# Partial sums of a five-tap convolution in a PSUM bank instead of SBUF

## The chip, the core and the metric

The kernel runs on one core of one Trainium2 chip. The metric is the device time of one execution in microseconds (us), and the median of three runs is compared. Four engines compute beside each other, each through its own queue in order: PE (matmuls, which write PSUM), DVE (element by element, reads and writes SBUF and PSUM), ACT (activations with a scale and a bias) and POOL (element by element, SBUF only). SP issues the DMAs. In the kernel's text they are `nc.tensor`, `V`, `A`, `P` and `nc.sync`.

## The reference

One layer of a hybrid block on x of 2048 x 1024 in float32. What the change touches is the centred depthwise convolution of the q, k and v columns:

```
mod = silu(c) @ ada_w + ada_b;  shift, scale, gate = split(mod)
h = rms_norm(x, norm_w) * (1 + scale) + shift
proj = h @ w_in                     # 1024 -> u 512, z_a 512, qkv 3 x 512, z_b 512, 16 gate columns
y_a = s5(u), gelu, GLU, * silu(z_a)           # diagonal state space, both directions
qkv = silu(conv(qkv, conv_w))       # 5 taps along the sequence, each channel by itself
q, k = l2_normalize(q) / sqrt(128), l2_normalize(k)
y_b = gated delta rule(q, k, v, g, beta), both directions, * silu(z_b)
out = rms_norm(x + gate * (concat(y_a, y_b) @ w_out), final_norm_w)
```

So for channel c and position t the convolution is the sum over j = 0..4 of conv_w[j, c] * raw[t + j - 2, c].

## The kernel before

The program has three stages. The first makes h, split into two float16 parts (`hhi`, `hlo`), and the four u column groups; the second, which is the one that matters here, makes the other columns of `proj` and the whole S5 scan beside them; the third runs the delta rule chunk by chunk with the GLU and the output projection beside it.

**The second stage.** `w_in` is taken in groups of 128 columns. A group is a *job* of four *iterations*, one per block of 512 positions. An iteration has one `gemm` on PE (24 matmuls of 128 x 512 into a bank with the tag `gm`) and one evacuation from that bank by ACT; then comes `tick()`, which emits what earlier iterations put off by `later(n, ...)`, and one step of the generator `side`, which is the S5 work. Nothing is reordered afterwards (`manual_schedule`): each engine's queue has the order in which the Python code emits. The jobs stand in the list `order` (line 182): z groups, the 16 gate columns, four k groups, four q groups, then v and z groups in turn.

**The convolution.** A k, q or v group goes through `conv_job`. With 512 positions of `raw` [128 channels x 2052 positions] written by ACT (L1017), these steps follow an iteration apart:

- `tap`: ACT writes a tile `cv` = conv_w[0] * raw (L1025);
- `conv`: DVE adds the taps 1 to 4 with four SCALAR_TENSOR_TENSOR (L1032), each `cv = raw[shifted] * conv_w[j] + cv`;
- `gated`: ACT applies silu in place (L1038) and squares (L1045);
- `total`, `taken`: PE sums the squares into a `pt` bank, DVE takes them (`kss` L1063 for k, `iq` L1059 for q);
- for k, after the fourth block, an inverse root of 13 small DVE operations (`rkt`, `rky`, `rk`), and then `turn` (PE transposes, L1075), `norm` (DVE, `kt`, L1085) and `back` (PE, L1092); for v only `turn`.

There are 12 such jobs, so 48 calls of `conv` and 192 SCALAR_TENSOR_TENSOR.

**The S5 work beside it.** At first it makes tables (`s5_tables`, eight times): POOL multiplies SBUF tiles (`bpw`, `cpw`, `tmp`; 12 operations of 128 x 512), PE transposes and multiplies into `sq` banks, ACT copies those out. Later come 16 batches of the scan, one step of `side` per iteration by turns: `s5_in` (PE into two `sq` banks, then four DVE products `w<-sq,rt`, then two POOL sums `w<-w,w`), and in the next iteration `s5_out` of the batch before (PE into two `sq` banks, `sq<-uT,tt` first, then ACT gelu) with `s5_scan` (four DVE scans `xs`, three DVE products, three POOL operations). POOL meanwhile makes `rt` tables for batches ahead.

**PSUM.** Eight banks: two with the tag `gm`, three `pt`, three `sq`. In this stage `sq` belongs to the S5 work alone. A tile is taken with `bank(tag)`, and whoever first writes it waits until the earlier user of that bank has been read to the end.

Of the kernel before, what the change touches and what calls it, by code (L numbers as in the profile page):

```python
# [31 lines left out]
def mm(nc, out, lhsT, rhs, start=True, stop=True):  # L32
    nc.tensor.matmul(out, lhsT, rhs, start=start, stop=stop)  # L33


def bc(ap, n):
    return ap.unsqueeze(2).to_broadcast([ap.shape[0], ap.shape[1], n])
# [3 lines left out]
def block(ctx, tc, x, c, ada_w, ada_b, norm_w, w_in, conv_w,  # L41
# [5 lines left out]
    V, A, P = nc.vector, nc.scalar, nc.gpsimd  # L47
# [39 lines left out]
    def bank(tag, shape=(128, 512)):  # L87
        return psum.tile(list(shape), F32, tag=tag, name=tag, bufs=PS_BUFS[tag])
# [19 lines left out]
    def rsqrt(pool, dst, src, tag):  # L108

        shp = list(src.shape)  # L110
        y = pool.tile(shp, F32, tag=tag + "y", name=tag + "y")
        t = pool.tile(shp, F32, tag=tag + "t", name=tag + "t")
        V.tensor_scalar(out=t.bitcast(I32), in0=src.bitcast(I32), scalar1=1, scalar2=None,
                        op0=ALU.arith_shift_right)
        V.tensor_scalar(out=y.bitcast(I32), in0=t.bitcast(I32), scalar1=-1.0,
                        scalar2=float(0x5F3759DF), op0=ALU.mult, op1=ALU.add)
        for it in range(3):
            V.tensor_tensor(out=t, in0=y, in1=y, op=ALU.mult)
            V.scalar_tensor_tensor(out=t, in0=t, scalar=-0.5, in1=src, op0=ALU.mult, op1=ALU.mult)
            V.scalar_tensor_tensor(out=(dst if it == 2 else y), in0=t, scalar=1.5, in1=y,  # L120
                                   op0=ALU.add, op1=ALU.mult)
# [52 lines left out]
    cw = s5t.tile([128, 12, 5], F32, name="cw")  # L174
# [798 lines left out]
    def later(n, fn, rank=0):  # L973
        late.append((clock[0] + n, fn, rank))
# [9 lines left out]
    def job(i, evac):  # L984
        w = w_done(i)
        for tb in range(NB):
            ps = gemm(w, tb)
            evac(tb, ps, w[2])
            if tb == 0:
                w_dma(i + 2)  # L990
                mx, cut = w_max(i + 1), w_cut(i + 1)
                next(mx, None)
            elif tb == 1:
                whole(mx)
            else:
                next(cut, None)
                next(cut, None)
            tick()
# [8 lines left out]
    def conv_job(i, kind, h):  # L1007
        i12 = kind * 4 + h
        raw = rp.tile([128, L + 4], F32, tag="big", name="raw")
        V.memset(raw[:, 0:2], 0.0)  # L1010
        V.memset(raw[:, L + 2:L + 4], 0.0)
        cvs = {}
        if kind == 1:
            ss, rk = [sp.tile([128, NCH], F32, tag=t, name=t, bufs=2) for t in ("kss", "rk")]

        def evac(tb, ps, iv):
            A.activation(out=raw[:, 2 + tb * 512:2 + (tb + 1) * 512], in_=ps, func=AF.Copy, scale=iv)  # L1017
            if tb:
                later(1, lambda: tap(tb - 1))
            if tb == NB - 1:  # L1020
                later(2, lambda: tap(tb))

        def tap(tb):
            cv = cvs[tb] = tp.tile([128, 512], F32, tag="cv", name="cv", bufs=9)
            A.activation(out=cv, in_=raw[:, tb * 512:tb * 512 + 512], func=AF.Copy, scale=cw[:, i12, 0:1])  # L1025
            later(1, lambda: conv(tb))

        def conv(tb):
            cv = cvs[tb]
            o = tb * 512  # L1030
            for j in range(1, 5):
                V.scalar_tensor_tensor(out=cv, in0=raw[:, o + j:o + j + 512], scalar=cw[:, i12, j:j + 1], in1=cv,  # L1032
                                       op0=ALU.mult, op1=ALU.add)
            later(1, lambda: gated(tb))

        def gated(tb):
            cv = cvs[tb]
            A.activation(out=cv, in_=cv, func=AF.Silu)  # L1038
            if kind == 0:
                nc.sync.dma_start(out=qT_d[:, tb * 4:tb * 4 + 4, h, :], in_=cv.rearrange("p (c t) -> p c t", t=128))  # L1040
            if kind == 2:
                later(1, lambda: turn(tb))
                return
            sq = tp.tile([128, 512], F32, tag="sq", name="sq")
            A.activation(out=sq, in_=cv, func=AF.Square)  # L1045
            later(1, lambda: total(tb, sq), 2)

        def total(tb, sq):

            ps = bank("pt")  # L1050
            for j in range(4):
                mm(nc, ps[:, j:j + 1], sq[:, j * 128:(j + 1) * 128], ones[:, 0:1])
            later(1, lambda: taken(tb, ps), 1)

        def taken(tb, ps):
            c4 = slice(tb * 4, tb * 4 + 4)
            if kind == 0:

                V.tensor_scalar(out=iq2[:, c4, h], in0=ps[:, 0:4], scalar1=EPS, scalar2=128.0 * EPS,  # L1059
                                op0=ALU.add, op1=ALU.mult)  # L1060
                cvs.pop(tb)
                return
            V.tensor_scalar(out=ss[:, c4], in0=ps[:, 0:4], scalar1=EPS, scalar2=None, op0=ALU.add)  # L1063
            if tb == NB - 1:

                rsqrt(sp, rk, ss, "rk")
                for n in range(NB):
                    later(1 + n, lambda n=n: turn(n), 2)

        def turn(tb):  # L1070
            c4 = slice(tb * 4, tb * 4 + 4)
            cv = cvs.pop(tb)
            ps = bank("pt")
            for j in range(4):
                nc.tensor.transpose(ps[:, j * 128:(j + 1) * 128], cv[:, j * 128:(j + 1) * 128], ident)  # L1075
            if kind == 2:
                vt = tp.tile([128, 4, 128], F32, tag="z", name="vt", bufs=3)
                A.activation(out=vt, in_=ps, func=AF.Copy)
                nc.sync.dma_start(out=vt_d[:, c4, h, :], in_=vt)
                return  # L1080
            later(1, lambda: norm(ps, c4), 1)

        def norm(ps, c4):
            kt = tp.tile([128, 4, 128], F32, tag="kt", name="kt", bufs=3)
            V.tensor_tensor(out=kt, in0=ps.rearrange("p (c d) -> p c d", d=128), in1=bc(rk[:, c4], 128), op=ALU.mult)  # L1085
            nc.sync.dma_start(out=kt_d[:, c4, h, :], in_=kt)
            later(2, lambda: back(kt, c4), 1.5)

        def back(kt, c4):
            ps = bank("pt")  # L1090
            for j in range(4):
                nc.tensor.transpose(ps[:, j * 128:(j + 1) * 128], kt[:, j, :], ident)  # L1092
            kk = tp.tile([128, 4, 128], F32, tag="z", name="kk", bufs=3)
            A.activation(out=kk, in_=ps, func=AF.Copy)
            nc.sync.dma_start(out=kT_d[:, c4, h, :], in_=kk)

        job(i, evac)
# [763 lines left out]
```

## Time and profile before

| | |
|---|---|
| median of 3 runs | 1428.95 us (1426.14 to 1430.29) |
| the profiled execution: time | 1428.77 us |
| its span, first to last instruction | 1427.1 us |
| its mean granted PE clock | 0.952 |
| busy in the span: PE, DVE, ACT, POOL | 1297.3, 1057.0, 672.9, 733.2 us |
| the taps (L1032), all 192 | 197.5 us of DVE, from 266.9 to 762 us |

The time lies 1.7 us over the span and 0.2 us under the median. The profile comes in views: the page (shares and the costliest groups of instructions), groups of instructions by line, one line's or tile's shortest, median and longest duration, the sum of each pair of "who waited for whom", stretches of the span with each engine's busy time, the instructions in order of time, and the chain of waits that ended last. A row of the page's groups reads: line, engine, operation, out<-in, shapes, count | busy us, mean ns | idle time just before them and what ended most of it. The granted PE clock is a share of full speed.

### The profile page before, as it was taken

The numbers are of one execution on the slowest core, as the hardware profiler recorded it, in microseconds if no ns is written. First come the engines' busy times: TensorE is split into PE (matmuls) and PEld (weight loads), VectorE is DVE, ScalarE is ACT, GpSimd is POOL, SyncE is SP. The second block draws the span as 40 slices with busy tenths as digits, with TensorE's granted clock in tenths as the row PEclk, the third lists the DMA queues.
The fourth block names the chain that finished last, engine by engine and source line by source line (L and its number), as shares of the span: only waits on it lengthen the run. The fifth ranks groups of instructions, "written<-read, shape, count | busy, mean of one in ns | idle before, by whom it ended". The sixth has DMA issues, their size and how long they took to land.

```text
span 1427.1 us, 26499 instructions
## 1 busy us (share of the span) xinstructions
PE 1297.3 (91%) x9936; PEld 907.2 (64%) x9936; DVE 1057.0 (74%) x2095; ACT 672.9 (47%) x1348; POOL 733.2 (51%) x680
## 2 busy tenths in 40 slices
PE   3879897797999998999999889999999988998997
PEld 2445343354565554555455578999999877886885
DVE  4645488988866799999984677887888665865664
ACT  4444321452455454353536666667667523433232
POOL 3223223685642367978761566655555125653543
PEclk9889998898999999999999899999999999999999
DMA  9455333122346623434324523543444489685533
GB/s 316 155 122 146 99 83 91 57 88 71 107 133 163 177 83 113 125 107 135 115 89 141 170 63 110 158 125 135 134 123 175 160 274 319 216 310 206 177 104 111
DMA packets 255280, 206.43 MB, mean 145 GB/s; under 512 B 88496, under 2 KB 206256, under 8 KB 255152
## 3 DMA queue, kind: packets, MB, share of 16 engines
q1 hardware_dynamic: 255152, 204.75, 46.4%
q8 instruction: 78, 1.28, 0.4%
q14 instruction: 50, 0.41, 0.1%
HBM read 133.38 MB, written 73.33 MB: 145 GB/s over the span
## 4 chain that ended last, share of the span: by engine, by line
PE 64%; DVE 21%; DMA 4%; issue 3%; ACT 3%; POOL 1%; SPq 1%; DVEq 0%; ACTq 0%; POOLq 0%
PE gm L33 36%; PE sq L33 15%; PE pt L33 12%; DVE cv L1032 6%; DVE w L510 2%; DMA y<-ya_d 1%; DVE xs L939 1%; DVE tm L510 1%; DVE wl L223 1%; PE pt L1075 1%; DVE t L510 1%; DMA kq<-qT_d 1%; DVE YT L1432 1%; DVE pb L1419 1%; PE sq L1748 1%
## 5 line engine op out<-in xcount | busy, mean ns | idle before, releaser
L33 PE MATMUL gm<-hhi,wh 128*128 128x512 f16 (+1 forms) x784 | 296.7, 394 | 13.0 <-ACT wh L221 6.9
L33 PE MATMUL gm<-hhi,wl 128*128 128x512 f16 (+1 forms) x784 | 294.9, 391 | 9.2 <-DVE wl L223 9.2
L33 PE MATMUL gm<-hlo,wh 128*128 128x512 f16 (+1 forms) x784 | 295.9, 393 | 0.0
L33 PEld LDWEIGHTS <-wh 128*128 128x128 f16 (+1 forms) x1664 | 154.4, 101 | 202.7 <-issue 30.9
L1032 DVE SCALAR_TENSOR_TENSOR cv<-raw,cw,cv 128x512 f32<-128x512 f32 x192 | 197.5, 1030 | 31.4 <-ACT cv L1025 26.3
L33 PEld LDWEIGHTS <-wl 128*128 128x128 f16 (+1 forms) x832 | 80.1, 100 | 109.2 <-DVE wl L223 12.6
L1017 ACT ACTIVATE raw<-gm,w 128x512 f32<-128x512 f32 x48 | 33.1, 689 | 180.9 <-PE gm L33 180.9
L510 POOL TENSOR_TENSOR w<-w,w 128x512 f32<-128x512 f32 x32 | 50.1, 1576 | 86.4 <-DVE w L510 86.4
L33 PE MATMUL gm<-yh,gwh 128*128 128x256 f32 x256 | 80.5, 315 | 6.7 <-ACT yh L778 5.4
L33 PE MATMUL gm<-yl,gwh 128*128 128x256 f32 x256 | 73.9, 289 | 0.7 <-POOL yl L779 0.7
L1770 POOL TENSOR_TENSOR r<-r,xt 128x512 f32<-128x512 f32 x32 | 41.5, 1297 | 62.2 <-DVE r L1769 29.1
L33 PE MATMUL gm<-yh,gwl 128*128 128x256 f32 x256 | 73.1, 285 | 0.0
L1440 ACT ACTIVATE Y<-pt 128x512 f16<-128x512 f32 x96 | 58.0, 604 | 24.5 <-PE pt L33 22.9
L939 DVE TENSOR_TENSOR_SCAN xs<-c,w 128x255 f32<-128x255 f32 x64 | 65.1, 1074 | 2.4 <-POOL w L510 2.4
L33 PE MATMUL sq<-S,kq 128*128 128x128 f32 x480 | 62.4, 282 | 0.0
L33 PEld LDWEIGHTS sq<-S,kq 128*128 128x128 f32 x480 | 60.0, 196 | 2.0
L1419 DVE CAST_PREDICATED pb<-msk,pt 128x512 f16<-128x512 int8 x80 | 57.0, 715 | 5.5 <-PE pt L33 4.4
L33 PE MATMUL pt<-Y,nh 128*128 128x64 f16 (+1 forms) x896 | 56.5, 198 | 4.6 <-DVE Y L1427 4.2
L320 POOL TENSOR_SCALAR hhi<-hf 128x512 f16<-128x512 f32 x32 | 30.1, 960 | 54.3 <-ACT hf L318 54.1
L1441 ACT ACTIVATE YT<-pt 128x512 f16<-128x512 f32 x96 | 57.3, 597 | 0.0
L33 PEld LDWEIGHTS <-nh 128*128 128x128 f16 x1024 | 48.2, 98 | 13.7 <-issue 6.6
L223 DVE SCALAR_TENSOR_TENSOR wl<-ws,w,wh 128x1024 f16<-128x1024 f32 (+1 forms) x25 | 36.2, 1448 | 27.6 <-ACT wh L221 27.6
(453 smaller groups left out, 3488.6 us busy)
## 6 DMA issues: line engine op xcount, KB each, us to landing
xt<-in_x_dram SPq DMA_DIRECT2D x25, 512.0 KB
ws<-in_w_in_dram SPq DMA_DIRECT2D x24, 512.0 KB
aw<-in_ada_w_dram SPq DMA_DIRECT2D x24, 512.0 KB
kq<-kT_d SPq DMA_DIRECT2D x32, 256.0 KB
kq<-qT_d SPq DMA_DIRECT2D x32, 256.0 KB
kt<-kt_d SPq DMA_DIRECT2D x32, 256.0 KB
vt<-vt_d SPq DMA_DIRECT2D x32, 256.0 KB
out_dram<-r SPq DMA_DIRECT2D x16, 512.0 KB
```

The source lines that it names most:

```text
L33: nc.tensor.matmul(out, lhsT, rhs, start=start, stop=stop)
L223: V.scalar_tensor_tensor(out=wl, in0=ws, scalar=s, in1=wh, op0=ALU.mult, op1=ALU.subtract)
L320: P.tensor_scalar(out=hhi[:, k, sl], in0=hf, scalar1=1.0, scalar2=1.0, op0=ALU.mult, op1=ALU.mult)
L510: (e or V).tensor_tensor(out=o, in0=a, in1=b, op=op)
L939: V.tensor_tensor_scan(out=o, data0=m1, data1=v, initial=0.0, op0=ALU.mult, op1=ALU.add)
L1017: A.activation(out=raw[:, 2 + tb * 512:2 + (tb + 1) * 512], in_=ps, func=AF.Copy, scale=iv)
L1032: V.scalar_tensor_tensor(out=cv, in0=raw[:, o + j:o + j + 512], scalar=cw[:, i12, j:j + 1], in1=cv, op0=ALU.mult, op1=ALU.add)
L1075: nc.tensor.transpose(ps[:, j * 128:(j + 1) * 128], cv[:, j * 128:(j + 1) * 128], ident)
L1419: V.copy_predicated(out=cols(PB[d][li], b, d), mask=mb, data=pp.rearrange("p t (n b) -> p t n b", b=b))
L1440: A.activation(out=cols(Y[d], b, d), in_=pa.rearrange("p t (n b) -> p t n b", b=b), func=AF.Copy)
L1441: A.activation(out=cols(YT[d], b, 1 - d), in_=pb.rearrange("p t (n b) -> p t n b", b=b), func=AF.Copy)
L1770: P.tensor_tensor(out=r[:, ns], in0=r[:, ns], in1=xt[:, ns], op=ALU.add)
```

## The change

`conv` takes a `sq` bank for each of its calls. Tap 1 reads `raw` and `cv` as before and writes the bank; taps 2 and 3 read `raw` and the bank and write the bank; tap 4 reads `raw` and the bank and writes `cv` in SBUF. Tap 0 by ACT (L1025) and everything behind `conv` stay.

```diff
         def conv(tb):
-            cv = cvs[tb]
+
+            cv, ps = cvs[tb], bank("sq")
             o = tb * 512
             for j in range(1, 5):
-                V.scalar_tensor_tensor(out=cv, in0=raw[:, o + j:o + j + 512], scalar=cw[:, i12, j:j + 1], in1=cv,
+                V.scalar_tensor_tensor(out=cv if j == 4 else ps, in0=raw[:, o + j:o + j + 512],
+                                       scalar=cw[:, i12, j:j + 1], in1=cv if j == 1 else ps,
                                        op0=ALU.mult, op1=ALU.add)
             later(1, lambda: gated(tb))
```

No instruction moves to another place or engine (behind the diff the line numbers are two higher). What changes is operands and waits. On DVE, at the second and third call of `conv` of the first k group (`kss` are the sums of squares, `w` a weight group's scale), before:

```order
L1010 MEMSET raw 128x2
L1011 MEMSET raw 128x2
L1032 SCALAR_TENSOR_TENSOR cv<-raw,cw,cv 128x512 [waits Activation_49]
L1032 SCALAR_TENSOR_TENSOR cv<-raw,cw,cv 128x512 [waits DVE_49] x3
L1063 TENSOR_SCALAR kss<-pt 128x4 [waits PE_49]
```

and with the change:

```order
L1010 MEMSET raw 128x2
L1011 MEMSET raw 128x2
L1033 SCALAR_TENSOR_TENSOR sq<-raw,cw,cv 128x512 [waits DVE_49,Activation_49]
L1033 SCALAR_TENSOR_TENSOR sq<-raw,cw,sq 128x512 [waits DVE_49] x2
L1033 SCALAR_TENSOR_TENSOR cv<-raw,cw,sq 128x512 [waits DVE_49]
L1065 TENSOR_SCALAR kss<-pt 128x4 [waits PE_49]
```

Each tap still waits for the one before it (DVE for itself); the first one now waits for the bank's earlier user too. On PE, at the start of `s5_out` of one batch (`uT`, `tt` and `cpt` are its inputs, `w` the scan's result), before:

```order
L33 MATMUL pt<-ones,sq 128x1 [waits DVE_49,Activation_49]
L33 MATMUL pt<-ones,sq 128x1 x3
L33 MATMUL sq<-uT,tt 128x256
L33 MATMUL sq<-uT,tt 128x256 [waits DVE_49,PE_49]
L33 MATMUL sq<-w_4813,cpt 128x256 [waits DMAHW4_49]
```

and with the change:

```order
L33 MATMUL pt<-ones,sq 128x1 [waits DVE_49,Activation_49]
L33 MATMUL pt<-ones,sq 128x1 x3
L33 MATMUL sq<-uT,tt 128x256 [waits DVE_49,PE_49]
L33 MATMUL sq<-uT,tt 128x256 [waits DVE_49]
L33 MATMUL sq<-w_4842,cpt 128x256 [waits DMAHW4_49]
```

With one of the three `sq` banks in the hands of `conv`, `s5_out` has to take both banks of the `s5_in` just before it, so its first matmul waits for DVE as well, where before only its second one did.

## The prediction

> **What bounds the kernel now.** The page gives the span and the group that the change touches, and the view by stretches says what its neighbourhood looks like. The columns of the latter: stretch, its length, busy time and count of PE, PE's weight loads, DVE, ACT and POOL, granted PE clock, share of the DMA engines, GB/s.
>
> ```profile
> span 1427.1 us, 26499 instructions
> L1032 DVE SCALAR_TENSOR_TENSOR cv<-raw,cw,cv 128x512 f32<-128x512 f32 x192 | 197.5, 1030 | 31.4 <-ACT cv L1025 26.3
> ...
> 480.00:570.00 90.00, 83.53 (x463) 46.80 (x462) 85.70 (x108) 41.85 (x69) 62.95 (x50) 0.94 0.33 99
> 570.00:710.00 140.00, 136.09 (x752) 71.65 (x752) 133.24 (x151) 62.72 (x101) 115.15 (x93) 0.98 0.39 117
> ```
>
> The taps lie between 266.9 and 762 us. There PE and DVE take turns as the bound: from 480 to 570 DVE is busy 85.7 of 90 us, from 570 to 710 PE is busy 136 of 140. A shorter DVE is therefore worth only what PE waits for it. The third view, PE's waits from 260 to 765 us (total us, times, longest):
>
> ```profile
> PE pt L1075 <- DVE kss L1063: 6.4, 2, 6.0
> PE gm L33 <- DVE wl L223: 6.1, 1, 6.1
> PE sq L33 <- DVE w L510: 5.2, 5, 3.1
> PE pt L33 <- DVE raw L1011: 3.0, 1, 3.0
> PE pt L1075 <- DVE iq L1059: 2.8, 1, 2.8
> PE pt L33 <- DVE iq L1059: 2.4, 1, 2.4
> PE pt L1075 <- DVE kt L1085: 1.9, 1, 1.9
> PE pt L1092 <- DVE kt L1085: 1.2, 1, 1.2
> ```
>
> All of them are for DVE, 29.0 us together. That is the frame: without its second-order effects the change cannot win more.
>
> **The change part by part.** *The four taps.* The fourth view, shortest/median/longest duration in ns by line, shows what a tap costs and why its mean of 1030 is so far over its median:
>
> ```profile
> L1032 DVE SCALAR_TENSOR_TENSOR cv<-raw,cw,cv x192: 740/752/1841, 266.9 to 761.2; 128x512 f32<-128x512 f32 x192
> L510 DVE TENSOR_TENSOR w<-sq,rt x64: 674/682/692, 483.2 to 742.8; 128x512 f32<-128x512 f32 x64
> L510 DVE TENSOR_TENSOR w<-xs,rt x32: 658/1040/1766, 494.4 to 751.6; 128x512 f32<-128x512 f32 x32
> L799 DVE SCALAR_TENSOR_TENSOR za<-gm,glub,za x32: 464/484/485, 810.4 to 1104.3; 128x256 f32<-128x256 f32 x32
> L1750 DVE SCALAR_TENSOR_TENSOR yb<-sq,dnw,zb x16: 739/744/752, 1200.5 to 1408.9; 128x512 f32<-128x512 f32 x16
> L510 POOL TENSOR_TENSOR bpw<-pwbr,bsi x7: 1054/1502/1506, 235.2 to 399.0; 128x512 f32<-128x512 f32 x7
> ```
>
> The same product in the same stage takes 674 to 692 ns in all 64 cases with one input in PSUM (`w<-sq,rt`), and 658 to 1766 with both inputs in SBUF (`w<-xs,rt`). POOL's operations, which read SBUF, stretch as well (1054 to 1506). So DVE and POOL get in each other's way where DVE reads two SBUF tiles, and not where one of them is in PSUM. Taps 2 to 4 change from the first kind to the second; tap 1 stays of the first. The chain of waits (start us, us) shows taps 2 to 4 of one call of `conv` in a collision, and from a later call one quiet tap:
>
> ```profile
> 313.98 1.65 DVE cv L1032
> ...
> 315.65 1.44 DVE cv L1032
> ...
> 317.11 1.43 DVE cv L1032
> ...
> 327.69 0.76 DVE cv L1032
> ```
>
> *What a tap will cost.* For reading PSUM the nearest row is `yb`: the same operation, size and kind of scalar, one input in PSUM, 744 against the tap's quiet 752; so nothing, or 8 ns less. No row shows a DVE write to PSUM, nor one that reads and writes the same bank. From below it is bounded by those 8 ns. From above I take once more all that an instruction costs beside its elements: 256 elements are 484 ns (`za`) and 512 are 744, so 260 per 256 elements, and 744 - 520 = 224 ns are fixed. I take nothing, because PSUM reading, the nearest row, costs nothing; both ends go into the range. A tap of the second kind is then 0.76 us with its gap, and a call like the one above saves 1.65 + 1.44 + 1.43 - 3 x 0.76 = 2.24 us.
>
> [...]
>
> *What the saving is worth, stall by stall.* Quiet calls save nothing. The calls behind PE's stalls, from the instructions in order of time:
>
> ```profile
> 266.88 5.34 DVE L1032 SCALAR_TENSOR_TENSOR cv<-raw,cw,cv 128x512 f32<-128x512 f32 x4
> 341.99 6.14 DVE L1032 SCALAR_TENSOR_TENSOR cv<-raw,cw,cv 128x512 f32<-128x512 f32 x4
> 377.45 6.14 DVE L1032 SCALAR_TENSOR_TENSOR cv<-raw,cw,cv 128x512 f32<-128x512 f32 x4
> 394.98 6.03 DVE L1032 SCALAR_TENSOR_TENSOR cv<-raw,cw,cv 128x512 f32<-128x512 f32 x4 [3.57 <-ACT cv L1025]
> ...
> 311.34 0.71 ACT L1025 ACTIVATE cv<-raw,cw 128x512 f32<-128x512 f32 x1
> ```
>
> - A, the 6.1 us for `wl` until 282.85: DVE works without a pause from the call at 266.88, which collides in taps 2 to 4: 2.2.
> - B, the 6.0 us for `kss` until 330.1: three colliding calls from 292 to 312 come before it, but PE waits for nothing there, and the fourth call cannot start before its tap 0 has left ACT at 311.34 + 0.71 = 312.05. So only the call of 312.49 counts, and the 0.4 by which it starts after 312.05: 2.6. Behind it come the 13 small operations of the inverse root.
> - C, 3.0 before 348.9 (call of 341.99): 2.2. D, 1.9 before 384.2 (call of 377.45): all 1.9. E, 1.2 before 401.7 (call of 394.98): all 1.2. What is late next in D and E is the evacuation of the `gemm` by ACT, which waits for PE itself.
> - F, 480 to 570, where DVE is the bound. Four calls recur (the row of 679 is for G, the last three are taps 2 to 4 of the call of 506.21):
>
> ```profile
> 485.85 4.52 DVE L1032 SCALAR_TENSOR_TENSOR cv<-raw,cw,cv 128x512 f32<-128x512 f32 x4
> 499.48 3.10 DVE L1032 SCALAR_TENSOR_TENSOR cv<-raw,cw,cv 128x512 f32<-128x512 f32 x4
> 506.21 4.94 DVE L1032 SCALAR_TENSOR_TENSOR cv<-raw,cw,cv 128x512 f32<-128x512 f32 x4
> ...
> 679.05 4.93 DVE L1032 SCALAR_TENSOR_TENSOR cv<-raw,cw,cv 128x512 f32<-128x512 f32 x4
> ...
> 508.00 1.00 DVE cv L1032
> 509.02 1.00 DVE cv L1032
> 510.05 1.10 DVE cv L1032
> ```
>
> The first saves 4.52 - 3.10 = 1.4 (its first tap is quiet), the second nothing, the third 1.00 + 1.00 + 1.10 - 3 x 0.76 = 0.8, the fourth collides in its first tap alone. Eight calls lie between 485 and 562: 2 x 2.2 = 4.4. PE's two waits for `iq`, 2.8 and 2.4, lie in this stretch and hold 5.2, so all of it counts.
>
> - G, the 3.1 for `w` until 697.5: one call like the third (4.93 us at 679) and one like the fourth: 0.8.
>
> The sum is 2.2 + 2.6 + 2.2 + 1.9 + 1.2 + 4.4 + 0.8 = 15.3 us, on 16 calls (one each in A, C, D, E, two in B, G, eight in F). The others, from 570 to 660 and from 710 on, lie beside PE at work; they save DVE time and no span. All taps together lie 197.5 - 192 x 0.752 = 53 us over their quiet time; three quarters of it, 40, are what DVE can save at most, so without PE's cover the others would be worth up to 25 us more.
>
> *The clock.* After a stall the `gemm` of 24 matmuls runs slower:
>
> ```profile
> 331.25 6.89 PE gm L33 x24
> ...
> 351.79 6.91 PE gm L33 x24
> ...
> 360.36 5.20 PE gm L33 x24
> ...
> 385.68 6.90 PE gm L33 x24
> ```
>
> The first, second and last stand behind B, C and D: 1.7 us each over the 5.20. C shrinks to 0.8 and D goes, B stays at 3.4. The two may be worth 3.4; I take 2.5.
>
> *The bank.* `conv` queues on DVE behind its tap 0 anyway; its bank was last used by itself, by DVE, or by S5 tiles that ACT read an iteration ago. So tap 1 does not wait. PE's first two matmuls of `s5_out`, 0.6 us, now stand behind the last of the four products of `s5_in` instead of before it:
>
> ```profile
> 523.85 0.68 PE L33 MATMUL sq<-uT,tt 128*128 128x256 f32 x2
> 524.75 0.67 PE L33 MATMUL sq<-uT,tt 128*128 128x256 f32 x2 [0.23 <-DVE w L510]
> ```
>
> That costs only where PE arrives before DVE is done, and where PE is the bound afterwards: at the ends of F and G and once near 630, 3 x 0.45 = 1.3. Behind these matmuls stand ACT's gelu and PE's next `gemm`; both are 0.45 later there, and nothing else waits for them.
>
> Together 15.3 + 2.5 - 1.3 = 16.5 us less than the profiled 1428.8: 1412.3. The median of the runs shown is 0.2 over it: 1412.5.
>
> **The rivals.** *The collisions move (1423).* POOL, no longer held up by taps, gets through its tables sooner and meets other DVE operations with two SBUF inputs: the scans, `w<-xs,rt`, the inverse root. For it: these stand right behind the taps in A, B and F. Against it: POOL also finishes sooner, so the total of shared time shrinks. If A, B and F give all back, 2.2 + 1.9 + 0.8 + 1.2 = 6.1 is left, less 1.3 for the bank and with 1 for the clock: 5.8, 1423.
>
> *A tap inside one bank is slow (slower, 1441).* If taps 2 and 3, which read and write one bank, take its elements twice (520 ns each) and a write costs the fixed 224 ns on three taps, a quiet call gets 1.7 us longer and a colliding one 0.5 shorter. Then A, C, D, E win 2.2; B loses 1.7 - 0.5 = 1.2; F loses 8 x 1.7 - 4.4 = 9.2; G loses 2 x 1.7 - 0.8 = 2.6; the bank 1.3: 12 us slower. It decides from 14 / 16 = 0.9 us per call. Against it: the `gemm` row above has PE add 24 times into one bank at 5.20 / 24 = 0.22 us per 512 columns, a reading and a writing each; DVE asks for less than half that pace.
>
> *More than the taps (1402).* POOL, less held up, leaves the neighbours alone: half of the 13.7 us of PE's waits that the sum leaves, 6.8, and all three slow `gemm`, 5.1: 15.3 + 6.8 + 5.1 = 27.2.
>
> *It does not do what it says (1430).* Taps 2 to 4 still read `raw` from SBUF and go on colliding: nothing but the bank's 1.3. The row `w<-sq,rt` speaks against it.
>
> **How the numbers follow.** The forecast (1405 to 1420) 0.60, collisions move 0.20, more 0.08, slow bank 0.07, no effect 0.05. The range reaches over the first and most of the second: 1404 to 1424; the upper bound of a PSUM write alone, 16 x 3 x 0.22 = 10.6, leads to 1423 and lies in it. A measurement here tells about 0.3%, 4.3 us, from no change, so faster is below 1424.7: 0.60 + 0.08 and 0.12 of the second case, 0.80. Same: 0.08 + 0.05 = 0.13. Slower: 0.07.
>
> **What would show it.** Taps 2 to 4 all near 750 ns with longest under 800, tap 1 still up to 1.8 us; DVE's tap time 40 us down at most, to 158, and rather less, since first taps collide oftener; POOL's longest `bpw` rows nearer to 1054. The stalls of C, D and E under 1 us and those of A and B at 3.9 and 3.4; 480 to 570 shorter by 4 to 5. PE's first `sq<-uT,tt` behind `w`. Wrong would be: taps 2 and 3 over 1 us without POOL at work, a wait of tap 1 for anything but ACT's tap 0, new waits of PE for taps, or stalls A to F as long as before with faster taps (then something else was the last to arrive).

## The result, and the profile after

The changed kernel takes 1407.01 us (median of 4 runs, 1399.43 to 1409.92) against 1427.55 (4 runs, 1423.39 to 1430.29) for the kernel before beside it: a ratio of 0.9852, 95% interval 0.9812 to 0.9892, or 15 to 27 us less. The prediction was 1412.5, with 1404 to 1424 as its range.

The profiled execution of the changed kernel is the fastest of its four, 1399.43 us. Where a size matters, the same kernel profiled once more is set beside it (called the repeat, 1408.24 us). First the taps, shortest/median/longest in ns, which answer to the row of L1032 before:

```profile
L1033 DVE SCALAR_TENSOR_TENSOR sq<-raw,cw,sq x96: 754/756/757, 268.5 to 730.2; 128x512 f32<-128x512 f32 x96
L1033 DVE SCALAR_TENSOR_TENSOR sq<-raw,cw,cv x48: 745/796/1844, 266.9 to 728.7; 128x512 f32<-128x512 f32 x48
L1033 DVE SCALAR_TENSOR_TENSOR cv<-raw,cw,sq x48: 747/748/749, 270.1 to 731.0; 128x512 f32<-128x512 f32 x48
```

Taps 2 and 3 (`sq<-raw,cw,sq`) and tap 4 (`cv<-raw,cw,sq`) have lost their spread altogether: the longest of 144 is 757 ns. Tap 1, which still reads two SBUF tiles, goes on colliding up to 1844. Next, PE's waits from 250 to 745 us (total us, times, longest):

```profile
PE gm L33 <- DVE wl L223: 6.0, 2, 5.1
PE pt L1077 <- DVE kss L1065: 3.9, 1, 3.9
PE sq L33 <- DVE cv L1033: 2.0, 2, 1.2
PE sq L33 <- DVE w L510: 1.9, 2, 1.2
PE pt L33 <- DVE raw L1011: 0.7, 1, 0.7
PE pt L1077 <- DVE iq L1061: 0.3, 1, 0.3
```

From 260 to 765 us, the stretch of the prediction's view, they are 13.9 us where there were 29.0 (0.9 of the first row lies ahead of it). Those of D and E (`kt`) are gone, those for `iq` in F nearly, C is at 0.7, G at most at 1.2; A and B are left at 5.1 and 3.9. The third row is new: PE waits for tap 4 to leave a bank. The `gemm` rows of the chain of waits that answer to those behind B, C and D (start us, us):

```profile
326.99 6.32 PE gm L33 x24
...
343.48 5.29 PE gm L33 x24
...
372.84 5.20 PE gm L33 x24
```

They were 6.89, 6.91 and 6.90. POOL's product `bpw<-pwbr,bsi`, which had a median of 1502, is quiet too:

```profile
L510 POOL TENSOR_TENSOR bpw<-pwbr,bsi x7: 1053/1055/1060, 234.6 to 384.1; 128x512 f32<-128x512 f32 x7
```

The quiet taps have not merely missed POOL's work. Before, 82 of the 192 taps took over 800 ns, all of them beside products of POOL (products of over 0.5 us, shared for over 0.2 us); of those not beside one, none took over 753. After, 67 of the 144 taps 2 to 4 still lie beside such products, and the longest of them took 757.

**Where the time went, by place.** The start of each iteration's `gemm` is a row of the trace; the difference of two such starts, before and after, says what the stretch between them won. From iteration 13 (250.43 us before) to iteration 80 (790.68), the second stage is 28.0 us shorter in the changed kernel and 25.2 in the repeat.

| place (iterations) | predicted | change | repeat |
|---|---|---|---|
| A, `wl` (13 to 18) | 2.2 | 0.85 | 0.6 |
| B, `kss` (18 to 23) | 2.6 | 2.1 | 2.5 |
| C (24 to 25) | 2.2 | 3.5 | 3.5 |
| a wait of 0.4 for `kss` (27 to 28) | 0 | 0.8 | 0.8 |
| D (28 to 29) | 1.9 | 2.1 | 2.1 |
| E (30 to 31) | 1.2 | 2.4 | 2.4 |
| F (44 to 51) | 4.4 | 6.7 | 4.1 |
| G (66 to 67) | 0.8 | 5.7 | 5.7 |
| slow `gemm` behind them | 2.5 | 5.4 | 4.5 |
| bank (55 to 56, 63 to 64) | -1.3 | -2.45 | -2.0 |
| a wait of 0.8 for `w` near 630 us (58 to 59) | 0 | 1.0 | 1.0 |
| sum | 16.5 | 28.0 | 25.2 |

The rest of the 29.3 between the two profiled executions, 1.3, lies ahead of iteration 13. The repeat is 20.5 us shorter in all: 25.2 in the stage, less 3.0 lost ahead of it and 1.6 behind iteration 80. The edit touches nothing there: these stretches differ by some us from one execution to the next. The kernel before was traced once, and some 2 us of the table are that execution's own, as the account of E in the section on why the prediction came out as it did shows.

### The profile page after: what moved, and what is told of

It is laid out like the page before. It is cut to its first block, busy times and chain, and to the rows that moved or that the text cites. A ratio compares the mean times of both kernels' runs of the same rounds, so it can differ in the third digit from the quotient of the medians.

```text
span 1397.7 us, 26524 instructions
## 1 busy us (share of the span) xinstructions
PE 1282.3 (92%) x9936; PEld 900.3 (64%) x9936; DVE 1017.6 (73%) x2095; ACT 672.5 (48%) x1348; POOL 708.1 (51%) x680
## 3 DMA queue, kind: packets, MB, share of 16 engines
q8 instruction: 78, 1.28, 0.4%
## 4 chain that ended last, share of the span: by engine, by line
PE 67%; DVE 16%; DMA 4%; issue 3%; POOL 3%; ACT 2%; SPq 1%; DVEq 0%; POOLq 0%; ACTq 0%
PE gm L33 37%; PE sq L33 15%; PE pt L33 12%; DVE sq L1033 2%; DVE w L510 2%; DVE tm L510 1%; DVE xs L939 1%; PE pt L1077 1%; POOL w L510 1%; DMA y<-ya_d 1%; DVE t L510 1%; PE sq L1750 1%; DMA xt<-in_x_dram 0%; DVE r L1782 0%; DVE cv L1033 0%
## 5 line engine op out<-in xcount | busy, mean ns | idle before, releaser
L1033 DVE SCALAR_TENSOR_TENSOR sq<-raw,cw,cv 128x512 f32<-128x512 f32 x48 | 55.2, 1151 | 29.6 <-ACT cv L1025 29.5
L1033 DVE SCALAR_TENSOR_TENSOR sq<-raw,cw,sq 128x512 f32<-128x512 f32 x96 | 72.6, 756 | 3.4
L939 DVE TENSOR_TENSOR_SCAN xs<-c,w 128x255 f32<-128x255 f32 x64 | 61.1, 1013 | 1.1 <-POOL w L510 1.1
L1003 ACT ACTIVATE z<-gm,w 128x512 f32<-128x512 f32 x32 | 22.0, 688 | 80.0 <-PE gm L33 48.0
```

Of the source, the lines that this page charges most:

```text
L939: V.tensor_tensor_scan(out=o, data0=m1, data1=v, initial=0.0, op0=ALU.mult, op1=ALU.add)
L1003: A.activation(out=z, in_=ps, func=AF.Silu, scale=iv)
L1033: V.scalar_tensor_tensor(out=cv if j == 4 else ps, in0=raw[:, o + j:o + j + 512], scalar=cw[:, i12, j:j + 1], in1=cv if j == 1 else ps, op ...
```

## The experiments

My theory: a tap is held up only while both it and an operation of POOL read SBUF with DVE reading two tiles there; taking one of DVE's inputs from PSUM ends that, and the price is what the bank costs. Rivals: it is the writing in place that matters, or any work of POOL; and for the path, that gains in one place are lost in another. All medians are beside runs of the kernel before on the same chip; "stage" is what the second stage won from iteration 13 to 80 in the profiled execution.

| form | median us | ratio, 95% interval | stage us |
|---|---|---|---|
| the change, repeated | 1405.0 | 0.9838, 0.9820 to 0.9855 | 25.2 |
| partial sums in a second SBUF tile | 1430.88 | 1.0025, 1.0012 to 1.0038 | 2.2 |
| taps in SBUF, bank taken anyway | 1432.69 | 1.0022, 1.0006 to 1.0038 | 0.0 |
| one immune tap | 1431.24 | 1.0028, 1.0015 to 1.0041 | 2.1 |
| one immune tap, bank kept | 1415.24 | 0.9900, 0.9872 to 0.9928 | 17.3 |
| POOL's table products as memsets | 1389.61 (one run) | | 35.2 |
| bank for k groups alone | 1414.86 | 0.9907, 0.9885 to 0.9929 | 16.8 |
| bank for q and v groups alone | 1420.63 | 0.9946, 0.9923 to 0.9969 | 14.0 |
| the change, bank kept | 1407.57 | 0.9846, 0.9821 to 0.9870 | 27.1 |
| tap 0 in the bank too | 1408.47 | 0.9849, 0.9827 to 0.9871 | 25.4 |
| tap 0 in the bank, k groups alone | 1401.98 | 0.9820, 0.9797 to 0.9843 | 31.6 |
| the same, bank kept for q and v | 1402.89 | 0.9814, 0.9789 to 0.9839 | 31.3 |

### The change, repeated

> The changed kernel once more, unaltered. It shows how far one execution's trace may be taken for all: the profiled one had 1399.4 us, its other runs 1406 to 1410. Expected: median 1403 to 1411, ratio to the kernel before 0.982 to 0.989. All 144 taps 2 to 4 at 747 to 757 ns again, whatever the total; a difference of the total then comes from stalls, not from taps. The rival, that the 1399 us were the rule and the others disturbed, expects a median under 1402.

The taps came out the same to the nanosecond (756, 748, first taps 1150 on average), the time 2 us lower. PE's waits for `wl` were 7.3 instead of 6.0 and those for `cv` 1.5 instead of 2.0, so an execution's own variation is about 1 us for a stall (in F, which holds several, 2.6).

### Is it the bank, or that the sum is not written in place?

```diff
-            cv, ps = cvs[tb], bank("sq")
+            cv, ps = cvs[tb], tp.tile([128, 512], F32, tag="pp", name="pp", bufs=1)
```

(and eight `cv` tiles instead of nine, to make room).

> The partial sums go to a tile of their own, but in SBUF (one buffer; the ring of cv has 8 in place of 9 to make room). Theory: a tap is held up because it reads two SBUF tiles while POOL reads SBUF, so a tile apart changes nothing: mean tap about 1030 ns, taps up to 1.6 us in positions 2 to 4, time within 0.3% of the kernel before (1423 to 1432 us). Rival: what cost was the sum in place (one tile read and written by one instruction); then the taps are near 750 ns and the time near 1407.

The groups of the taps, where `pp` is the second SBUF tile:

```profile
L1033 DVE SCALAR_TENSOR_TENSOR pp<-raw,cw,pp x96: 750/752/1652, 270.4 to 758.9; 128x512 f32<-128x512 f32 x96
...
L1033 DVE SCALAR_TENSOR_TENSOR cv<-raw,cw,pp x48: 750/752/1630, 273.5 to 759.7; 128x512 f32<-128x512 f32 x48
```

Taps 2 to 4 still collide, and tap 1 (between the two rows) with them; nothing is won. It is where the second input lies, not what is overwritten.

### What the bank alone costs

The four taps as before, all in SBUF, and two one-element writes of DVE into the bank, one ahead of the taps and one behind them:

```diff
+            V.tensor_scalar(out=ps[:, 0:1], in0=cw[:, i12, 0:1], scalar1=1.0, scalar2=None, op0=ALU.mult)
             for j in range(1, 5):
-                V.scalar_tensor_tensor(out=cv if j == 4 else ps, in0=raw[:, o + j:o + j + 512],
-                                       scalar=cw[:, i12, j:j + 1], in1=cv if j == 1 else ps,
+                V.scalar_tensor_tensor(out=cv, in0=raw[:, o + j:o + j + 512], scalar=cw[:, i12, j:j + 1], in1=cv,
                                        op0=ALU.mult, op1=ALU.add)
+            V.tensor_scalar(out=ps[:, 1:2], in0=cw[:, i12, 0:1], scalar1=1.0, scalar2=None, op0=ALU.mult)
```

> The taps stay in SBUF as before; conv takes an sq bank all the same, writes one element of it ahead of tap 1 and one behind tap 4 (two extra DVE operations of about 0.1 us per call). It measures the bank's loss from the rotation alone. Theory (the prediction's term): 1.3 us for PE's matmuls that stand behind conv's or s5_in's bank, and the 16 calls on the path bring 16 x 0.2 = 3 us with the extra operations: 1428 to 1434 us. Rival (the loss of a bank costs more than stated, and the gain of the taps is larger than the net result): 1436 us or more.

The interval of 0.06 to 0.38% over the kernel before is 1 to 5 us, the two small operations included (the one behind the taps took 147 to 155 ns). PE's waits show for what:

```profile
PE sq L33 <- DVE sq L1036: 6.0, 3, 3.6
```

So the bank's price is PE waiting for the end of a convolution that DVE has not reached. With colliding taps DVE is later, and the price higher, than in the change (2.0). The stage's 0.0 hides this: 2.3 us are lost at iteration 55, 4.2 at 63 and 1.3 at 64, and 5.7 are won at G, where the wait for `w` is gone because PE arrives later and not because DVE is faster. That a wait has gone is therefore no proof of faster taps; for G the form below that keeps one bank decides, which has no wait for a bank and wins the same 5.7.

### Does one immune tap do a third of it?

Tap 1 writes the bank, tap 2 reads it, taps 3 and 4 stay in SBUF; the bank is taken a call at a time, as in the change:

```diff
-                V.scalar_tensor_tensor(out=cv if j == 4 else ps, in0=raw[:, o + j:o + j + 512],
-                                       scalar=cw[:, i12, j:j + 1], in1=cv if j == 1 else ps,
+                V.scalar_tensor_tensor(out=ps if j == 1 else cv, in0=raw[:, o + j:o + j + 512],
+                                       scalar=cw[:, i12, j:j + 1], in1=ps if j == 2 else cv,
```

> Tap 1 writes the bank, tap 2 reads it and writes cv, taps 3 and 4 stay in SBUF. Theory: only a tap with an input in PSUM is immune, so tap 2 is at 745 to 760 ns in all 48 calls, taps 3 and 4 still collide (up to 1.6 us), mean over all four near 950. Since 2 of the 3 collisions stay, a third to a half of the gain: 1415 to 1422 us. Rival (the gain comes from the sum leaving SBUF as such, writes included): taps 3 and 4 get quiet too and the time is near 1407.

This missed. Tap 2 was immune (746 to 749 ns), taps 3 and 4 collided (mean 899), and by iteration 45 the kernel had won 9 us; at iteration 66 it was 3 behind. PE's waits say why, and one of them in PE's and DVE's rows:

```profile
PE sq L33 <- DVE cv L1033: 17.3, 6, 6.0
```

```profile
511.96 1.98 PE L33 MATMUL sq<-uT,bpt 128*64 128x256 f32 x8 [5.96 <-DVE cv L1033]
```

```profile
501.89 3.63 DVE L939 TENSOR_TENSOR_SCAN xs<-c,w 128x255 f32<-128x255 f32 x4
...
509.39 1.74 DVE L1033 SCALAR_TENSOR_TENSOR sq<-raw,cw,cv 128x512 f32<-128x512 f32 x1
511.16 0.75 DVE L1033 SCALAR_TENSOR_TENSOR cv<-raw,cw,sq 128x512 f32<-128x512 f32 x1
```

PE's second `s5_in` tile has the bank that this convolution uses, and starts when tap 2 has read it, at 511.91. DVE came to that convolution only after 7.6 us of scan and products. The bank that a tile gets is settled when the program is built, by the order in which the banks come free in its text. The order in the v groups (the numbers are banks, c marks a call of `conv`, the others are S5's tiles):

```
the change:       5c 4 5 3c 5 4 3c 5 4 3c 4 5 3 4 5 4 3
one immune tap:   5c 5 3 4c 3 5 4c 4 3 5c 3 4 5 3 4 3 5
```

With the bank free two taps earlier, the next S5 tile is given the very bank of the convolution before it (`5c 5`), in place of one that was free long since (`5c 4`).

The test of that reading keeps one bank for all 48 calls, so that none of S5's tiles ever gets it:

```diff
+    mine = []
...
+            if not mine:
+                mine.append(bank("sq"))
+            ps = mine[0]
```

> The form with one immune tap (tap 1 writes the bank, tap 2 reads it, taps 3 and 4 stay in SBUF), which had come out at 1431 with PE waiting 17.3 us for cv before its next tile in an sq bank; here the bank is taken once and kept for all 48 calls, so S5 never gets a bank that a tap still has to read. Theory (the 17.3 us came from which tile gets the early freed bank, not from the taps): those waits are gone, taps 3 and 4 collide as they did (mean about 900), and the 8 us that were won by iteration 45 stay: 1416 to 1422. Rival (one tap in the bank is worth nothing on the path, whichever bank): 1427 to 1432.

No wait of PE for `cv` is left, taps 3 and 4 collide as before (mean 901), and 1415.24 comes out, 0.8 under the theory's range. So one immune tap of three is worth 15 us, two thirds of the change, and all of it had been lost to who gets which bank.

### Is it POOL's reading?

The kernel before, with all taps in SBUF; in the S5 tables each of POOL's products is a memset of the same tile. The products of those tables are left out.

```diff
             for i in range(2):
+                if e is P:
+                    for u in (o[i], t, o[i]):
+                        P.memset(u, 0.01)
+                    continue
                 TT(o[i], a[0], b[i], ALU.mult, e)
```

> The form before (all taps in SBUF), with one thing changed: in the S5 table stage each of POOL's products of two 128x512 SBUF tiles is replaced by a memset of the same output tile, so POOL writes the same tiles at the same places and reads none. It leaves the products of the S5 tables out of the computation. Theory (a tap is held up where both it and POOL's operation READ two SBUF tiles): the 76 taps between 262 and 425 us, mean 1109 ns before, come down to about 755 (up to 800, for the few other POOL operations that stay), and the k part gets 13 to 17 us shorter, about 1411 to 1416 in all. Rival (any POOL work or POOL writing of SBUF stretches DVE): taps that lie beside a memset stay over 900 ns. Since a memset may be much shorter than a product (1.05 to 1.5 us), only taps beside a memset decide between the two, the total does not.

The taps from 255 to 425 us (98 of them; shortest/median/longest), and one call of four, whose first three taps have POOL's memsets of 0.52 us beside them, until 257.39:

```profile
L1036 DVE SCALAR_TENSOR_TENSOR cv<-raw,cw,cv x98: 743/752/1097, 255.2 to 424.4; 128x512 f32<-128x512 f32 x98
```

```profile
255.23 3.11 DVE L1036 SCALAR_TENSOR_TENSOR cv<-raw,cw,cv 128x512 f32<-128x512 f32 x4 [0.61 <-ACT cv L1029]
```

Of the 98 taps, 36 overlap a memset by more than 0.2 us, and the longest of these took 754 ns. Four are over 760, 991 to 1097 ns, and all four lie beside the products of 128x256 that POOL still had to do:

```profile
395.73 4.27 DVE L1036 SCALAR_TENSOR_TENSOR cv<-raw,cw,cv 128x512 f32<-128x512 f32 x4 [1.42 <-ACT cv L1029]
```

```profile
395.64 0.61 POOL L510 TENSOR_TENSOR qh<-rtA,rtB 128x256 f32<-128x256 f32 x1
...
398.38 1.07 POOL L510 TENSOR_TENSOR qh<-rtA,rtB 128x256 f32<-128x256 f32 x1
```

POOL's product is stretched as well: the first `qh`, which had begun before the taps, took 0.61 us, the second 1.07. So POOL's writing harms no tap (754 ns at most beside memsets); its products, which read SBUF as well, do (991 to 1097 ns beside those of 128x256), though not in every case: 17 more taps lie beside POOL's products of 128x16 (`l`, `lks`) and took at most 752 ns. There POOL alone paid, up to 0.71 us for a product that takes 0.22 elsewhere.

The total missed: 1389.6 against 1411 to 1416. The stage won 35 us, and the small DVE operations, which collide as well, have a part in it. Two of the inverse root's (it has eleven in the trace, not 13), before, and the first of them here (ns):

```profile
L118 DVE TENSOR_TENSOR rkt<-rky x12: 174/176/1128, 320.8 to 426.0; 128x16 f32<-128x16 f32 x12
...
L115 DVE TENSOR_SCALAR rky<-rkt x4: 175/577/979, 319.7 to 424.5; 128x16 int32<-128x16 int32 x4
```

```profile
L118 DVE TENSOR_TENSOR rkt<-rky x12: 174/175/176, 297.2 to 385.6; 128x16 f32<-128x16 f32 x12
```

An operation of 16 elements a row takes up to 950 ns longer beside POOL's products. The four long ones of `rkt` began 0.1 to 0.2 us behind the start of a product and ended 0.02 to 0.03 us behind its end, so they waited it out. `rky<-rkt` reads one SBUF tile and collides too, up to 979 ns before and 175 here: two SBUF inputs are what makes a tap collide, but not the only thing that makes a DVE operation collide. I had counted only taps. POOL's work is shorter as well (0.52 us for a memset where its products took 1.05 to 1.5), and what that alone is worth was not shown, so this run's total is no measure of the collisions alone.

### The k groups, and the q and v groups

```diff
-            cv, ps = cvs[tb], bank("sq")
+            cv, ps = cvs[tb], bank("sq") if kind == 1 else None
```

with `kind != 1` for the second form; without a bank the taps go as before.

> The bank for the partial sums in the four k groups alone (16 of 48 calls); q and v groups as before. Theory (each of the stalls A to E shrinks by what its own calls save, and the S5 stretch behind takes the lead over unchanged): 12 to 15 us of the gain are there by 410 us, the stretch from 480 on is as before, total 1412 to 1416. Rival (a lead won early is taken back in the stretch where DVE is the bound, as it was with one tap in the bank): 12 us at 410 us, but DVE waits longer there for nothing it can do, PE waits for it from 480 to 570, and the total is 1420 to 1427.

> The reverse: the bank in the q and v groups (32 calls), the k groups as before. Theory (stalls add up independently): nothing up to 400 us, then 4 to 7 us from 480 to 570 (F) and 5 to 6 us at the w products before 697 (G), less about 1 us for the bank: 8 to 11 us, total 1416 to 1419; together with the k groups' result the sum of the two gains is within 3 us of the whole change's 22. Rival (the gains depend on each other): the two sums differ from 22 by more than 5 us.

The two gains are 13.0 and 7.2 us by the medians, 20.2 together, against 22.1 for the change repeated; by the profiled stages 16.8 and 14.0, against 25.2 to 28.0. The profiled execution of the second form is at that form's median, 1420.63, so its smaller gain in the whole lies outside the stage (3.0 lost ahead of it and 2.9 behind). Its 1420.63 is 1.6 over the theory's range; the sum of the two gains is within the 3 us that the theory allowed, and by the stages 2.8 to 5.6 more than the change's. Some 2 of that is what the traced execution of the kernel before lost by itself (see E below), which counts in both. The waits of PE in the two forms stand each where its own groups are:

```profile
PE sq L33 <- DVE w L510: 4.7, 3, 3.1
...
PE pt L1077 <- DVE iq L1061: 2.8, 1, 2.8
```

```profile
PE gm L33 <- DVE wl L223: 7.0, 2, 6.1
PE pt L1077 <- DVE w L143: 6.0, 1, 6.0
```

With the bank for k alone, waits of F and G are those of the kernel before to the tenth (2.8 for `iq`, 3.1 for `w`), and the lead of 15.2 us that it has won by iteration 33 is 15.4 at iteration 51: a lead won early is not taken back. With the bank for q and v alone, A and B stand as before (6.1, and 6.0 in B's place).

### The bank kept, and tap 0 in the bank

*The change, bank kept for all 48 calls* (the same three lines as above).

> The change with one difference: one sq bank is taken at the first call of conv and kept for all 48, so S5 has the other two to itself, and no PE work ever waits for a tap; only DVE touches that bank, in its own order. Theory (what the shared bank costs is PE's waits for the last tap, 1.5 to 2.0 us, and about 1 us of them reaches the end): PE's waits for cv on sq banks are gone, taps as before (754 to 757, 748), PE waits a little longer for ACT or w with two banks, as it does now; 1402 to 1406. Rival (S5 needs the third bank: its pairs of PE tiles wait for the readers of the last pair): new waits of PE's sq tiles for DVE's w products or ACT's gelu over 5 us, 1409 to 1415.

PE's waits for `cv` are gone, and no wait for `w` or ACT grew (`w` 2.6 as in the repeat). The time, 1407.57, is 1.6 over the theory's range and not told from the change's: in the medians, the bank's price is too little to see. In the traces it can be read off. The repeat and this form agree in every iteration of the stage to 0.02 us but for 55 and 63, where the repeat is 0.99 longer each: 2.0 us, the difference between 25.2 and 27.1.

*Tap 0 in the bank too*, so that no DVE tap reads two SBUF tiles:

```diff
-            A.activation(out=cv, in_=raw[:, tb * 512:tb * 512 + 512], func=AF.Copy, scale=cw[:, i12, 0:1])
+            pss[tb] = bank("sq")
+            A.activation(out=pss[tb], in_=raw[:, tb * 512:tb * 512 + 512], func=AF.Copy, scale=cw[:, i12, 0:1])
```

> The change with ACT's tap 0 in the bank as well, so that all four DVE taps have one input in PSUM. Theory by the collisions alone: tap 1 falls from a mean of 1150 to about 756, 19 us less DVE time than in the change, the k part gains 2 to 4 us more; 1399 to 1403. Rival (bank release): each bank is now held from tap 0 to tap 4, an iteration longer, and where DVE is the bound (480 to 570 us before) PE's S5 tiles wait for taps that lag: PE waits for cv over 6 us there and the total is 1408 to 1425. I hold the rival likelier, 0.6 to 0.4.

All 192 taps are quiet now (742 to 758 ns), and PE waits for banks instead:

```profile
PE sq L33 <- DVE cv L1034: 6.7, 4, 5.0
PE sq L33 <- DVE iq L1062: 5.2, 2, 3.8
```

DVE is 19.3 us less busy with taps than in the change (144.4 against 163.7), and the kernel is no faster: 6.7 + 5.2 us of waits ahead of S5's tiles, the longest at a table's matmuls at 275 us, and the next, 3.8 put down to `iq`, until 484.8 in the stretch where DVE is the bound; there DVE ends a tap 4 at 484.67 and the `iq` behind it 0.1 later. The rival's mechanism came at the place that it named and in the tables as well, at the low end of its range.

*Tap 0 in the bank for the k groups alone*, with the change's form for q and v:

```diff
+            if kind == 1:
+                pss[tb] = bank("sq")
-            A.activation(out=cv, in_=raw[:, tb * 512:tb * 512 + 512], func=AF.Copy, scale=cw[:, i12, 0:1])
+            A.activation(out=pss.get(tb, cvs[tb]), in_=raw[:, tb * 512:tb * 512 + 512], func=AF.Copy, scale=cw[:, i12, 0:1])
```

> The same in the four k groups alone, where S5 asks for few sq banks; q and v groups as in the change (tap 0 in SBUF). Theory: the 16 first taps of the k part fall from about 1130 to 756, 6 us less DVE time there, of which the stalls for wl (7.3 in the run repeated) and for the k sums (3.9) give back 1.5 to 3; no PE waits for cv over 2 us; 1402 to 1404. Rival (those stalls hang on other collided operations, the weight split wl<-ws,w,wh at 1.5 us a piece and the small operations of the inverse root): no difference, 1404 to 1408.

```profile
PE gm L33 <- DVE wl L223: 4.2, 2, 3.3
...
PE pt L1080 <- DVE w L143: 1.6, 1, 1.6
```

A's and B's waits are down to 3.3 and 1.6 and the stage wins 31.6 us, 3.6 more than the change: part of what A and B still cost there was tap 1.

*The last two forms together.*

> The two better forms together: tap 0 of the four k groups in the bank too, and for the q and v groups one sq bank taken once and kept. Theory (what is left of PE's waits for taps, 1.9 us behind cv in the form with tap 0 of k in the bank, goes, and the k part gains as it did there, some 31 us from iteration 15 to 80): PE waits for cv under 1 us, 1399 to 1403. Rival (the remaining waits for cv lie beside others and cost nothing; the gain of the k part was one execution's luck): 1403 to 1408, like the change itself.

1402.89 with 31.3 us of stage: the k part's gain came a second time. PE's waits for `cv` are 0.4 and 0.8. These two forms stand 2 to 5 us under the change, in medians 1401.98 and 1402.89 against 1405.0 and 1407.01; their intervals overlap with the change's, so that they are faster than the kernel before is shown, that they are faster than the change is likely and not settled.

## Why the prediction came out as it did

**The taps: right.** 2 to 4 were predicted at the quiet 752 and measured at 754 to 757 and 748; tap 1 was said to collide on, and does, but not oftener: 22 of 48 first taps took over 800 ns before and after, with means of 1152 and 1151. The PSUM write, taken as nothing between -8 and +224 ns, costs 4 ns, and the read of tap 4 saves 4. The rival of the slow bank falls with that. DVE's tap time, predicted at 158 or rather over it, is 163.7 (72.6 + 55.2 + 35.9): of the 53 us of collisions first taps held 19, over a third, and not the quarter that the prediction gave them.

**The stalls B and D: right in size. C: too small.** The prediction charged each place with what its taps save, and put the clock into the `gemm` rows alone. Those rows ran at a granted clock of 0.76, 0.76 and 0.75 behind B, C and D (6.89, 6.91 and 6.90 us), and at 1.00 in the row of 5.20. But what PE runs between the wait and the `gemm` is slow as well. C in PE's rows, before and after:

```profile
348.88 1.83 PE L33 MATMUL pt<-ones,sq 128*128 128x1 f32 x8 [2.97 <-DVE raw L1011]
350.64 0.72 PE L33 MATMUL sq<-cpw,bbr 64*32 64x128 f32 x16
```

```profile
341.82 1.02 PE L33 MATMUL pt<-ones,sq 128*128 128x1 f32 x8 [0.75 <-DVE raw L1011]
342.77 0.50 PE L33 MATMUL sq<-cpw,bbr 64*32 64x128 f32 x16
```

The wait shrank by 2.22, the predicted 2.2. From its end to the next `gemm` (351.79 before, 343.48 after) the small matmuls took 2.91 (granted clock 0.50) and now 1.66 (1.00), another 1.25, which makes the 3.5. What the clock term lacked is these small matmuls, 1.25 in C and 1.8 in G. For the two `gemm` that it counted, behind C and D, it was near: 2.5 taken of a possible 3.4, and 1.6 + 1.7 = 3.3 measured. The one behind B, which it left out, gave 0.6 in the change and 0.06 in the repeat.

**E: right in size, but the table has more.** The wait of 1.2 went, and 2.4 is measured, as the small matmuls behind it were slow in the traced execution of the kernel before (3.56 us up to the next `gemm` at a granted clock of 0.66, and 2.50 at 1.00 in the change). But in three forms whose k taps collide as before (bank for q and v alone, second SBUF tile, bank taken anyway) the wait is still there, 1.2 to 1.3, and these matmuls run quickly: the iteration is 1.0 shorter without any change to its taps. So 1.0 of the 2.4 is that execution's and not the change's. The same holds for the `gemm` behind E (0.5), which is as quick with the bank taken anyway, and for those behind F and G (0.6 or 0.2, and 0.4), which are as quick with a second SBUF tile. Whether matmuls behind a wait run slowly varies, then, from one execution to the next; what decides it was not tried.

**G: the largest miss, 5.7 for 0.8.** PE before and after, from the S5 output's first matmuls to the next `gemm`:

```profile
693.79 0.60 PE L33 MATMUL sq<-uT,tt 128*128 128x256 f32 x2
697.54 1.19 PE L33 MATMUL sq<-uT,tt 128*128 128x256 f32 x2 [3.15 <-DVE w L510]
698.66 3.78 PE L33 MATMUL sq<-w,cpt 64*128 64x256 f32 x16
702.38 0.61 PE L33 MATMUL gm<-hhi,wh 128*128 128x512 f16 x1
```

```profile
670.58 1.03 PE L33 MATMUL sq<-uT,tt 128*128 128x256 f32 x4
671.54 2.00 PE L33 MATMUL sq<-w,cpt 64*128 64x256 f32 x16
673.47 0.39 PE L33 MATMUL gm<-hhi,wh 128*128 128x512 f16 x1
```

8.59 us became 2.89. The wait of 3.15 went entirely; 1.8 more are the sixteen matmuls at half the pace (3.78 and 2.00 us, at granted clocks of 0.50 and 1.00), and the rest is the first four. With one bank kept, where PE waits for no bank, the place wins the same 5.7, so it is the taps that win it. The prediction let the wait shrink by one call's 0.8, since it looked at the calls of 679 and 691. The backlog of DVE before that wait is longer, though:

```profile
661.50 4.71 DVE L939 TENSOR_TENSOR_SCAN xs<-c,w 128x255 f32<-128x255 f32 x4 [2.04 <-POOL w L510]
...
670.40 5.10 DVE L1032 SCALAR_TENSOR_TENSOR cv<-raw,cw,cv 128x512 f32<-128x512 f32 x4
...
695.51 2.48 DVE L510 TENSOR_TENSOR w<-sq,rt 128x512 f32<-128x512 f32 x4
```

```profile
634.88 4.75 DVE L939 TENSOR_TENSOR_SCAN xs<-c,w 128x255 f32<-128x255 f32 x4 [0.19 <-POOL w L510]
...
667.52 2.48 DVE L510 TENSOR_TENSOR w<-sq,rt 128x512 f32<-128x512 f32 x4
```

DVE's last free moment is the wait ahead of the scan at 661.50. From there to the products is 34.0 us before and 32.6 after, 1.4 less, with three calls on the way; and the scan itself starts earlier against PE, 3.65 ahead of the `gemm` at 665.15 before and 6.06 ahead of that at 640.94 after, 2.4 more. Together 3.8, enough for all of the 3.15. (In the change PE also comes 1.0 later to this place, for a wait of 0.8 for the bank in iteration 63, and DVE waits 0.6 for PE on the way; with the bank kept neither is there, and the 34.0 come down to 31.9.) So the call of 670 and the time ahead of the backlog were left out.

**A: too large, 2.2 for 0.6 to 0.85.** The step itself was right: from the first tap to the end of `wl` DVE took 281.51 + 1.28 - 266.88 = 15.9 us, and takes 279.21 + 1.28 - 266.87 = 13.6, 2.3 less.

```profile
250.41 1.43 DVE L223 SCALAR_TENSOR_TENSOR wl<-ws,w,wh 128x1024 f16<-128x1024 f32 x1 [0.96 <-ACT wh L221]
...
281.51 1.28 DVE L223 SCALAR_TENSOR_TENSOR wl<-ws,w,wh 128x1024 f16<-128x1024 f32 x1
```

```profile
249.10 1.44 DVE L223 SCALAR_TENSOR_TENSOR wl<-ws,w,wh 128x1024 f16<-128x1024 f32 x1 [0.96 <-ACT wh L221]
...
266.87 1.63 DVE L1033 SCALAR_TENSOR_TENSOR sq<-raw,cw,cv 128x512 f32<-128x512 f32 x1
...
279.21 1.28 DVE L223 SCALAR_TENSOR_TENSOR wl<-ws,w,wh 128x1024 f16<-128x1024 f32 x1
```

But the first tap starts 16.5 us behind the `wl` of iteration 13 in the first profile and 17.8 in the second. In the form with a second SBUF tile, whose taps won nothing, it is 17.8 too, so these 1.3 us are not the change's doing: the profile of before had this stretch short. They are two small operations ahead of the tap, 0.18 and 0.58 us in the first profile (`su<-su,t`, `w<-w,ih`) and 1.09 and 0.96 in the second. What makes them quick in one execution and slow in another was not tried. Part of the rest was tap 1: with tap 0 in the bank A gives 2.7 and 2.5.

**F: right within what varies.** 4.4 predicted; 6.7, 4.1, and 4.1 with the bank kept.

**The bank: too small, and the account wrong.** -1.3 was predicted for PE's S5 matmuls standing behind the products, at the ends of F and G and near 630; nothing was lost there (near 630, 1.0 was won, with the bank kept too). Tap 1 waits for nobody, as said. The loss, 2.45 and 2.0, came from the other side: PE waits for tap 4, which the prediction named only as a sign against itself.

```profile
583.17 0.75 DVE L1033 SCALAR_TENSOR_TENSOR cv<-raw,cw,sq 128x512 f32<-128x512 f32 x1
```

```profile
583.97 1.08 PE L33 MATMUL sq<-uT,bpt 128*64 128x256 f32 x8 [1.24 <-DVE cv L1033]
```

Tap 4 ends at 583.92, and PE starts 0.05 later. "Its bank was last used by itself, by DVE, or by S5 tiles" looked at who is ahead of the taps and not at who is behind them.

**The rivals.** Collisions that move would have left A, B and F where they were; B and F won their part. Nor did the collisions move on the whole: from iteration 13 to 80 DVE's busy time without the taps is 257.5 us before, 253.9 in the change and 254.7 in the repeat, and POOL's is 329.8, 305.8 and 304.9. The rival "more than the taps" (1402) lies near the measured time and is right only in part: two of the three slow `gemm` went, and the waits that shrank did so by the taps, with C and D at 2.2 and 1.9 as worked out. The neighbours were left alone by some 3 us of 257 only; `rkt<-rky` of the inverse root still takes up to 1133 ns. The sum was short in the end: 16.5 predicted, 20.5 and 22.1 by the medians, 25 to 28 in the stage. That it came within 4 to 6 us is partly luck, as A was 1.4 to 1.6 too large, the bank 0.7 to 1.2 too cheap and G 4.9 too small.

## What to carry to other kernels

Where DVE and POOL work beside each other, look at the spread of a DVE operation and not at its mean: one that goes from 750 to 1850 ns with two SBUF inputs, beside POOL products, is quiet when one input lies in PSUM (757 at most), and the PSUM access costs 4 ns of 752 at most. Price the bank by who gets it next: when it is freed earlier or held longer, the order of the banks can eat the whole gain (17.3 us here), and a bank that one loop keeps to itself settles that. When a wait of PE goes, expect more from the work behind it, the small matmuls as well as the `gemm` (1.25 and 1.6 us in C), but do not count on it: the matmuls behind the wait of E took 1.0 us less in three other executions that had the same wait. Follow DVE's backlog back to its last free moment before saying which calls stand before a wait.

## What the runs showed that was not expected

- A DVE operation of 128x16 takes 175 ns, and up to 1128 beside POOL's products; with memsets in place of those, all twelve took 174 to 176. A small operation pays nearly as much in its worst collision (953 ns) as a tap (1089): the four long ones of `rkt` waited out POOL's product and ended 0.02 to 0.03 us behind its end.
- POOL pays in the same collisions: `qh<-rtA,rtB` takes 1.07 us beside taps and 0.61 where it began before them.
- After a wait of 3.15 us PE's matmuls ran at half pace at least from 697.54 to 702.78, 5.2 us, at a granted clock of 0.50. The sixteen of `w` and `cpt` among them took 3.78 us, and 2.00 in the change at a clock of 1.00.
- Two executions of the change have the same quiet taps (756 and 748 ns), and their second stages still differ by 2.8 us.
